# The second MLP product as seven block products in place of eight, with weight sums formed by accumulating DMAs

## The chip, the cores and the metric

One core of one Trainium2 chip runs the whole program. The metric is the time of the execution on the device in microseconds. The median of three runs of the kernel before is 1993.25 us (1992.52 to 1994.31).

## What is computed

Six layers work on 256 tokens of width 1024, in float32. Two come from a first block (three attention mixers side by side), four from a second (retention, conformer convolution, short convolution, retention). Each layer is a mixer and then an MLP that has the same shape in all six: 1024 to 4096, squared ReLU, 4096 back to 1024.

```python
# first block, for each of 2 layers
u = rmsnorm(x, ln2_g[layer]) @ w_up[layer]
x = x + jnp.square(jax.nn.relu(u)) @ w_down[layer]

# second block, for each of 4 layers
h = squared_relu_mlp(rms_norm(x, norm_g[i, 2]), mlp_w1[i], mlp_w2[i])
x = x + rms_norm(h, norm_g[i, 3])

def squared_relu_mlp(x, w1, w2):
    return jnp.square(jax.nn.relu(x @ w1)) @ w2
```

## The kernel before

**Precision.** Every large product is made of three matmuls. Each operand is split into a part `hi`, rounded to the type float32r, and a rest `lo`; the products hi·hi, hi·lo and lo·hi are summed in PSUM (`xs` and `ws`, lines 743 to 780). So a weight tile that has landed in a buffer `raw` is first cast by ScalarE (ACT) into `whi`, and VectorE (DVE) subtracts to get `wlo` (`prefetch`, lines 712 to 727). `hilo` (line 801) does the same for activations.

**Weights.** The host packs all weights into one tensor `in_w` in the order in which they are used (`plan`, line 69, and `pack`, line 1625), in units of up to 128 rows by 1024 columns, 512 KB each. SyncE issues one DMA for each unit. There are 4 buffers `raw` and 8 each of `whi` and `wlo`, each handed out in order (`CAPS`, line 41).

**The MLP** (`mlp`, line 1202). The token rows are two blocks of 128 (`t`), the output columns two halves of 512. The first four blocks of the hidden dimension come out with tokens on the partitions and are transposed. Then the loop over `p` from 2 to 15 runs: two units of the up projection give the hidden blocks 2p and 2p+1 with the hidden dimension on the partitions (`ws`, 48 matmuls of 256 columns into a PSUM bank `pu`); ReLU, square and hi/lo split follow on ACT and DVE; and the blocks 2p-4 and 2p-3 of the down projection are added up in four banks `acc` (`both`, 24 matmuls of 512 columns: 2 blocks x 2 token blocks x 2 column halves x 3). There are 14 such passes in each of six MLPs, 84 in all. `tail` (line 786) then does the last four hidden blocks, token block by token block and half by half, so that what follows a finished half (`Fin._half`, line 564: add to `x`, or a norm's sum of squares and gain) runs while the next half is being computed.

**PSUM.** Of eight banks four have the name `acc` and four `wk`.

**The order of the work.** The program is recorded first. A planner (`Rec.schedule`, line 389) then simulates all engines with the costs of `Rec.cost` (line 293), gives every instruction a due time from TensorE's order, and hands out buffers; the order that comes of this is emitted, one in-order stream for each engine (`Rec.emit`, line 536; so nearly all rows of the trace carry line 546). The planner's figures are its own; they are not measured times.

## Time and profile before

| | us |
|---|---|
| median of 3 runs | 1993.25 |
| span of the profiled execution, first to last instruction | 1991.4 |
| TensorE busy in it | 1949.0 (98%) |
| VectorE busy | 1335.8 (67%) |
| ScalarE busy | 1051.1 (53%) |
| GpSimd busy | 159.1 (8%) |
| moved by DMA | 341.44 MB, 52.6% of 16 engines' time on the main queue |

Only the span of the profiled execution is recorded, so times are set against the median by what lies between 1991.4 and 1993.25, 1.85 us. PE stands for the matmuls of TensorE, PEld for its loads of the stationary operand, DVE for VectorE, ACT for ScalarE, POOL for GpSimd, SP for SyncE, which issues the DMAs. Busy time is the union of an engine's instructions, so back-to-back matmuls of 394 ns each that overlap count less than their sum. `acc` and `wk` are PSUM banks; `t4k`, `r2k`, `s2k`, `s1k` are SBUF buffers of 4, 2, 2 and 1 KB on each partition.

### The profile page before, as it was taken

What the parts mean: (1) busy time and instruction counts of PE and PEld (TensorE: products, weight loads), DVE (VectorE), ACT (ScalarE), POOL (GpSimd) and SP (SyncE); (2) the same over time, 40 slices, a digit from 0 to 9 for tenths busy, and PEclk for the clock granted to TensorE, in tenths of its full rate; (3) what the DMA queues carried; (4) which work ended last, traced back from release to release, by engine and by line L of the source; (5) the groups of instructions that cost most, each with busy time, mean ns of one, the idle gap of its engine ahead of it and who ended that gap; (6) DMA issues with size and microseconds to landing.
All of it is one profiled execution on the core that took longest, in us unless ns stands there. A gap on an engine that the chain in (4) does not pass through costs nothing.

```text
span 1991.4 us, 30668 instructions
## 1 busy us (share of the span) xinstructions
PE 1949.0 (98%) x11696; PEld 1721.8 (86%) x11696; DVE 1335.8 (67%) x2169; ACT 1051.1 (53%) x1757; POOL 159.1 (8%) x233
## 2 busy tenths in 40 slices
PE   8999999999999999999997799999999999999998
PEld 7879998878998888899877689989899889888997
DVE  7866556886556776755589975567755577757554
ACT  7555545555545335645486655455545453555452
POOL 2200002100000000000047400000000000000000
PEclk9999999999999999999998899999999999999999
DMA  7256664246555555465631265646465655455552
GB/s 238 85 168 204 188 197 146 76 152 208 189 198 183 174 165 192 165 198 189 210 129 48 80 226 186 200 159 217 164 202 189 201 170 169 160 192 178 191 184 91
DMA packets 95763, 341.44 MB, mean 171 GB/s; under 512 B 10624, under 2 KB 10880, under 8 KB 95616
## 3 DMA queue, kind: packets, MB, share of 16 engines
q1 hardware_dynamic: 95616, 339.49, 52.6%
q8 instruction: 91, 1.49, 0.3%
q14 instruction: 56, 0.46, 0.1%
HBM read 338.40 MB, written 1.05 MB: 170 GB/s over the span
## 4 chain that ended last, share of the span: by engine, by line
PE 90%; DVE 6%; issue 1%; POOL 1%; DMA 1%; ACT 1%; SPq 0%; POOLq 0%; DVEq 0%; ACTq 0%
PE wk L546 47%; PE acc L546 43%; DVE s1k L546 4%; DVE s2k L546 1%; POOL s2k L546 1%; DMA raw<-in_w 1%; ACT s2k L546 0%; DVE wlo L546 0%; DMA x<-in_x 0%; DVE col L546 0%; DVE t4k L546 0%; DVE dg L546 0%; POOL s1k L546 0%; ACT whi L546 0%; SPq L546 0%
## 5 line engine op out<-in xcount | busy, mean ns | idle before, releaser
L546 DVE TENSOR_TENSOR wlo<-raw,whi 128x1024 fp32r<-128x1024 f32 (+3 forms) x639 | 774.0, 1217 | 538.2 <-ACT whi L546 533.6
L546 ACT CAST whi<-raw 128x1024 fp32r<-128x1024 f32 (+3 forms) x639 | 656.5, 1034 | 734.7 <-PE wk L546 374.5
L546 PE MATMUL wk<-t4k,whi 128*128 128x256 f32 x3712 | 662.8, 282 | 12.4 <-DVE s2k L546 8.8
L546 PEld LDWEIGHTS wk<-t4k,whi 128*128 128x128 f32 x3712 | 573.8, 190 | 22.0 <-DVE s2k L546 9.6
L546 PE MATMUL wk<-t4k,wlo 128*128 128x256 f32 x1856 | 510.7, 282 | 0.0
L546 PE MATMUL acc<-whi,r2k 128*128 128x512 f32 x1440 | 410.3, 394 | 0.0
L546 PE MATMUL acc<-whi,t4k 128*128 128x512 f32 (+2 forms) x1312 | 391.4, 387 | 5.9 <-ACT t4k L546 2.1
L546 PEld LDWEIGHTS wk<-t4k,wlo 128*128 128x128 f32 x1856 | 346.6, 190 | 0.1
L546 PEld LDWEIGHTS acc<-whi,r2k 128*128 128x128 f32 x1440 | 264.8, 188 | 54.6
L546 PEld LDWEIGHTS acc<-whi,t4k 128*128 128x128 f32 x1312 | 239.7, 189 | 48.5 <-ACT t4k L546 3.2
L546 PE MATMUL acc<-wlo,r2k 128*128 128x512 f32 x720 | 227.8, 393 | 0.0
L546 PE MATMUL acc<-wlo,t4k 128*128 128x512 f32 (+2 forms) x656 | 227.7, 386 | 0.0
L546 PE MATMUL wk<-whi,t4k 128*128 128x512 f32 x512 | 163.9, 398 | 0.0
L546 PEld LDWEIGHTS acc<-wlo,r2k 128*128 128x128 f32 x720 | 135.2, 188 | 31.1
L546 PEld LDWEIGHTS acc<-wlo,t4k 128*128 128x128 f32 x656 | 123.1, 190 | 20.1
L546 POOL TENSOR_TENSOR col<-col,mhalf 128x1 f32<-128x1 f32 (+1 forms) x48 | 38.3, 806 | 1157.1 <-DVE col L546 1156.8
L546 PEld LDWEIGHTS wk<-whi,t4k 128*128 128x128 f32 x512 | 95.8, 188 | 21.8 <-ACT t4k L546 0.4
L546 PE MATMUL wk<-wlo,t4k 128*128 128x512 f32 x256 | 98.7, 395 | 0.0
L546 PE MATMUL wk<-s2k,s2k 128*128 128x64 f32 (+6 forms) x492 | 85.3, 308 | 4.1 <-DVE s2k L546 3.6
L546 PEld LDWEIGHTS wk<-s2k,s2k 128*128 128x128 f32 (+2 forms) x492 | 72.6, 197 | 16.5 <-DVE s2k L546 4.0
L546 ACT ACTIVATE t4k<-wk,cv 128x128 fp32r<-128x128 f32 x256 | 72.4, 379 | 16.2 <-PE wk L546 15.9
L546 DVE SCALAR_TENSOR_TENSOR t4k<-wk,cv,t4k 128x128 fp32r<-128x128 f32 x256 | 72.4, 343 | 10.5 <-ACT t4k L546 9.6
(126 smaller groups left out, 1366.2 us busy)
## 6 DMA issues: line engine op xcount, KB each, us to landing
raw<-in_w SPq DMA_DIRECT2D x599, 512.0 KB, 4.2
raw<-in_w SPq DMA_DIRECT2D x26, 384.0 KB, 3.2
row<-in_rows SPq DMA_DIRECT2D x11, 512.0 KB, 5.0
raw<-in_w SPq DMA_DIRECT2D x8, 288.0 KB, 2.8
raw<-in_w SPq DMA_DIRECT2D x4, 432.0 KB, 4.8
kcs<-in_kc SPq DMA_DIRECT2D x2, 768.0 KB, 7.4
x<-in_x SPq DMA_DIRECT2D x4, 256.0 KB, 6.3
out_dram<-x SPq DMA_DIRECT2D x4, 256.0 KB, 2.0
```

Of the source, the lines that this page charges most:

```text
L546: op.dma = fn(*[res(a) for a in op.args], **{k: res(a) for k, a in op.kw.items()})
```

## The change

In the loop over `p` the pair of down blocks (2p-4, 2p-3) is no longer eight block products (two token blocks, two hidden blocks, two column halves) but seven, in Winograd's form of Strassen's algorithm. Each is three matmuls of 512 columns, 21 in place of 24. The seven results stay in seven PSUM banks over all 14 passes of an MLP (`strassen`), and are combined once at its end (`combine`, two copies and eight additions or subtractions). The last four hidden blocks still go through `tail` into four fresh banks, and what `combine` gave is added in `Fin` (`add`, `_half`).

The activations need four sums of the four blocks (`forms`); the blocks and sums, seven of 128 x 128, are split into hi and lo. The square is now taken on ACT.

The weights of a pair need seven forms of 128 x 512 each. `seven` makes them in one buffer `raw`: a DMA from SyncE loads two forms (512 KB), then DMAs issued by GpSimd with `accum_op=ALU.add` add further blocks of the weights to what lies in the buffer. Between these steps the buffer is split into `whi` and `wlo`, 1024, 1024, 1024 and 512 columns. There are four accumulating DMAs of 256 KB and one plain one of 256 KB beside the 512 KB load for each pair.

All eight banks get one name, `ps`. There are 6 buffers `raw`, handed out in any order, as `whi` and `wlo` now are; `dg`, the conformer's diagonal matrices, lie in `raw` buffers. The planner's costs change: matmuls by `n * 0.4434 + 4.5` ns, 1100 ns for a DMA issue on GpSimd, 4000 ns for a DMA in the due times, and the diagonals are made at most 6 us ahead.

```diff
@@ -29,6 +29,8 @@
 HALVED = 1
+DIAG_HOLD = 6000.0
+DMA_LAG = 4000.0
@@ -38,9 +40,9 @@
 SLACK = {}
-CAPS = {"raw": (4, True), "whi": (W_BUFS, True), "wlo": (W_BUFS, True), "t4k": (8, False), "row": (2, True),
+CAPS = {"raw": (6, False), "whi": (W_BUFS, False), "wlo": (W_BUFS, False), "t4k": (8, False), "row": (2, True),
         "s2k": (14, False), "r2k": (8, False), "s1k": (14, False), "col": (28, False), "keep": (20, False), "sm": (1, True),
-        "kcs": (1, True), "dg": (4, False), "acc": (4, False), "wk": (4, False)}
+        "kcs": (1, True), "ps": (8, False)}
...
@@ -62,7 +65,7 @@
     for p in range(2, 16):
-        out += u(p) + d(p - 2)
+        out += u(p) + [(down, l, (2 * p - 4, 2 * p - 3), SEVEN)]
...
@@ -295,7 +299,7 @@
             op.dma = n / 360.0
-            return 60.0, 2000.0
+            return (60.0 if op.eng == "sync" else 1100.0), 2000.0
@@ -305,7 +309,7 @@
             f32 = op.kw["lhsT"].vt.dtype == F32
-            return ((4 if f32 or n < 256 else 1) * max(n, P)) / 2.4 + 2.5, lat
+            return (4 * max(n, 64) / 2.4 + 5.0 if f32 else n * 0.4434 + 4.5), lat
@@ -331,10 +335,13 @@
         op.rush = self.rush
+        op.hold = self.hold
         op.label = sys._getframe(2).f_code.co_name if LABEL else ""
         items = [(k, a) for k, a in enumerate(args)] + list(kw.items())
         outs = [a for k, a in items if isinstance(a, V) and k in (0, "out", "accum_out")]
         ins = [a for k, a in items if isinstance(a, V) and k not in (0, "out", "accum_out")]
+        if "accum_op" in kw:
+            ins = ins + outs
@@ -380,7 +387,7 @@
                 q = ops[p]
-                lag = q.cost + (700.0 if q.dma else latency(q.eng, op.eng)) + q.dma
+                lag = q.cost + (DMA_LAG if q.dma else latency(q.eng, op.eng)) + q.dma
...
@@ -554,6 +561,17 @@
         self.parts = [[None, None], [None, None]]
+        self.part = None
+
+    def add(self, c):
+        net, nc = self.net, self.net.nc
+        if self.g is not None:
+            self.part = c
+            return
+        for t in range(2):
+            for hf in range(2):
+                x = net.x[t][:, hf * 512:hf * 512 + 512]
+                nc.vector.scalar_tensor_tensor(x, c[t][hf], self.scale[t], x, op0=ALU.mult, op1=ALU.add)
@@ -575,6 +593,10 @@
         else:
+            if self.part is not None:
+                y = self.part[t][hf]
+                nc.vector.tensor_add(y, y, p)
+                p = y
...
@@ -706,13 +728,16 @@
 
-    def ps(self, tag="wk"):
-        return VT(self.rec, tag, [P, 512], F32, True).view()
+    def ps(self):
+        return VT(self.rec, "ps", [P, 512], F32, True).view()
 
     def prefetch(self, upto):
         nc = self.nc
         while len(self.loaded) < min(upto, len(self.plan)):
             i = len(self.loaded)
+            if self.plan[i][3] is SEVEN:
+                self.loaded[i] = self.seven(i)
+                continue
@@ -726,10 +751,37 @@
 
+    def seven(self, i):
+        nc = self.nc
+        src = self.wpack[self.offs[i]:self.offs[i + 1]].rearrange("(p f) -> p f", p=P)
+        r = self.t("raw", [P, 1024])
+        out = []
+
+        def split(n):
+            hi = self.t("whi", [P, 1024], F32R)
+            lo = self.t("wlo", [P, 1024], F32R)
+            self.hilo(hi[:, :n], lo[:, :n], r[:, :n])
+            out.extend((hi[:, c:c + 512], lo[:, c:c + 512]) for c in range(0, n, 512))
+
+        nc.sync.dma_start(r, src[:, :1024])
+        split(1024)
+        for c in (slice(0, 512), slice(512, 1024)):
+            nc.gpsimd.dma_start(r[:, c], src[:, 1024:1536], accum_op=ALU.add)
+        split(1024)
+        nc.gpsimd.dma_start(r[:, :512], src[:, 512:1024], accum_op=ALU.add)
+        nc.sync.dma_start(r[:, 512:], src[:, 1536:2048])
+        split(1024)
+        nc.gpsimd.dma_start(r[:, :512], src[:, 1536:2048], accum_op=ALU.add)
+        split(512)
+        return out
+
     def unit(self, name, l, kbs):
         u = self.plan[self.wi]
         assert u[:3] == (name, l, tuple(kbs)), (u, name, l, kbs)
         self.prefetch(self.wi + 1 + LOOKAHEAD)
+        if u[3] is SEVEN:
+            self.wi += 1
+            return self.loaded[self.wi - 1]
@@ -783,11 +835,48 @@
 
-    def tail(self, items, acc, fin, first=False):
+    def forms(self, g):
+        nc = self.nc
+        e = self.t("s2k", [P, 4, P])
+        hi = self.t("t4k", [P, 7, P], F32R)
+        lo = self.t("t4k", [P, 7, P], F32R)
+        nc.vector.tensor_sub(e[:, 0:2, :], g[:, 0:1, :].to_broadcast([P, 2, P]), g[:, 1:3, :])
+        nc.vector.tensor_sub(e[:, 2, :], e[:, 1, :], g[:, 1, :])
+        nc.vector.tensor_add(e[:, 3, :], e[:, 2, :], g[:, 3, :])
+        self.hilo(hi[:, 0:3, :], lo[:, 0:3, :], g[:, 1:4, :])
+        self.hilo(hi[:, 3:7, :], lo[:, 3:7, :], e)
+        return [(hi[:, q, :], lo[:, q, :]) for q in range(7)]
+
+    def strassen(self, w, x, m, first, last):
+        f1, f5, f2, f6, f3, f7, f4 = w
+        xa1, xb2, xb1, s3, s1, s2, s4 = x
+        for b, (xh, xl), (wh, wl) in ((0, xa1, f1), (2, s4, f5), (4, s1, f2), (6, s3, f6), (5, s2, f3), (1, xb1, f7), (3, xb2, f4)):
+            self.mm(m[b], xh, wh, first, False)
+            self.mm(m[b], xh, wl, False, False)
+            self.mm(m[b], xl, wh, False, last)
+
+    def combine(self, m):
+        nc = self.nc
+        c = [[self.t("s2k", [P, 512]) for _ in range(2)] for _ in range(2)]
+        u2 = self.t("s2k", [P, 512])
+        u3 = self.t("s2k", [P, 512])
+        m1, m2, m3, m4, m5, m6, m7 = m
+        nc.scalar.copy(u2, m1)
+        nc.vector.tensor_add(u2, u2, m6)
+        nc.vector.tensor_sub(u3, u2, m7)
+        nc.vector.tensor_add(c[0][0], u3, m4)
+        nc.vector.tensor_sub(c[0][1], m5, u3)
+        nc.scalar.copy(c[1][0], m1)
+        nc.vector.tensor_add(c[1][0], c[1][0], m2)
+        nc.vector.tensor_sub(c[1][1], m5, u2)
+        nc.vector.tensor_add(c[1][1], c[1][1], m3)
+        return c
+
+    def tail(self, items, acc, fin, first=False, both=True):
         half = [slice(0, 512), slice(512, 1024)]
         for t in range(2):
             ts_ = slice(t * P, (t + 1) * P)
-            for hfs in ([(0, 1)] if first and t == 0 else [(0,), (1,)]):
+            for hfs in ([(0, 1)] if first and both and t == 0 else [(0,), (1,)]):
...
@@ -1204,7 +1293,7 @@
         px = [self.ps(), self.ps()]
-        h0 = [self.t("t4k", [P, 4, S], F32R) for _ in range(2)]
+        g0 = [self.t("s2k", [P, 4, P]) for _ in range(2)]
@@ -1213,26 +1302,38 @@
                 nc.tensor.transpose(pt[:, b * P:(b + 1) * P], r[:, b * P:(b + 1) * P], self.ident)
-            ts_ = slice(t * P, (t + 1) * P)
-            self.hilo(h0[0][:, :, ts_], h0[1][:, :, ts_], pt.rearrange("p (k n) -> p k n", k=4))
-        hT = {b: (h0[0][:, b, :], h0[1][:, b, :]) for b in range(4)}
-        acc = self.acc4()
+            for q in range(2):
+                for b in range(2):
+                    nc.scalar.copy(g0[q][:, 2 * b + t, :], pt[:, (2 * q + b) * P:(2 * q + b + 1) * P])
+        x = {q: self.forms(g0[q]) for q in range(2)}
+        m = None
+        hT = {}
         for p in range(2, 16):
             pu = self.ps()
             for j in range(2):
                 self.ws(self.unit(up, l, ALL), xT, pu[:, j * S:(j + 1) * S])
             r = self.t("s2k", [P, 512])
-            hh = self.t("r2k", [P, 512], F32R)
-            hl = self.t("r2k", [P, 512], F32R)
             nc.scalar.activation(r, pu, AF.Relu)
-            nc.vector.tensor_mul(r, r, pu)
-            self.hilo(hh, hl, r)
-            for j in range(2):
-                hT[2 * p + j] = (hh[:, j * S:(j + 1) * S], hl[:, j * S:(j + 1) * S])
-            for k in (2 * p - 4, 2 * p - 3):
-                self.both(self.unit(down, l, (k,)), [hT[k]], acc, k == 0)
+            if p < 14:
+                g = self.t("s2k", [P, 4, P])
+                nc.scalar.activation(g.rearrange("p a b -> p (a b)"), r, AF.Square)
+            else:
+                hh = self.t("r2k", [P, 512], F32R)
+                hl = self.t("r2k", [P, 512], F32R)
+                nc.vector.tensor_mul(r, r, pu)
+                self.hilo(hh, hl, r)
+                for j in range(2):
+                    hT[2 * p + j] = (hh[:, j * S:(j + 1) * S], hl[:, j * S:(j + 1) * S])
+            if m is None:
+                m = [self.ps() for _ in range(7)]
+            self.strassen(self.unit(down, l, (2 * p - 4, 2 * p - 3)), x.pop(p - 2), m, p == 2, p == 15)
+            if p < 14:
+                x[p] = self.forms(g)
+        c = self.combine(m)
+        acc = self.acc4()
         fin = mkfin(acc)
-        self.tail([(self.unit(down, l, (k,)), hT[k]) for k in range(28, 32)], acc, fin)
+        fin.add(c)
+        self.tail([(self.unit(down, l, (k,)), hT[k]) for k in range(28, 32)], acc, fin, first=True, both=False)
...
@@ -1408,7 +1509,8 @@
                 if (c, k0) not in kept:
-                    kept[c, k0] = dg = self.t("s2k" if n < S else "dg", [P, 4, P])
+                    self.rec.hold = DIAG_HOLD
+                    kept[c, k0] = dg = self.t("s2k" if n < S else "raw", [P, 4, P])
...
@@ -1627,6 +1730,11 @@
         w = inp[name][l]
+        if cs is SEVEN:
+            (a, b), h = kbs, 512
+            w = w.reshape(-1, P, 1024)
+            pieces.append(np.concatenate([w[a, :, :h], w[b, :, h:], w[a, :, h:], w[b, :, :h]], axis=1).ravel())
+            continue
...
```

## Rows read from the trace of the kernel before

**Rows 1.** The page, part 1: busy time of each engine, share of the span.

```profile
PE 1949.0 (98%) x11696; PEld 1721.8 (86%) x11696; DVE 1335.8 (67%) x2169; ACT 1051.1 (53%) x1757; POOL 159.1 (8%) x233
```

**Rows 2.** The page, part 4: the chain that ended last, by engine.

```profile
PE 90%; DVE 6%; issue 1%; POOL 1%; DMA 1%; ACT 1%; SPq 0%; POOLq 0%; DVEq 0%; ACTq 0%
```

**Rows 3.** That chain, last MLP: start us, us, what.

```profile
1822.12 5.55 PE acc L546 x24
1827.67 5.67 PE wk L546 x48
1833.34 5.52 PE acc L546 x24
...
1968.08 11.08 PE acc L546 x48
```

**Rows 4.** Waits of PE over the span: us in total, times, longest us.

```profile
PE wk L546 <- DVE s2k L546: 14.5, 4, 4.5
PE wk L546 <- DVE s1k L546: 8.4, 5, 3.7
PE wk L546 <- DMA x<-in_x: 4.6, 2, 4.0
```

**Rows 5.** Stretches: busy us by engine, clock, DMA share, GB/s.

```profile
core 0: us, PE busy (x) PEld busy (x) DVE busy (x) ACT busy (x) POOL busy (x), PEclk, DMA share, GB/s
8.00:16.00 8.00, 7.67 (x33) 6.49 (x34) 5.75 (x17) 7.26 (x20) 1.07 (x2) 1.00 1.02 404
630.00:720.00 90.00, 90.00 (x553) 80.41 (x552) 69.45 (x118) 39.85 (x56) 7.69 (x9) 1.00 0.53 175
...
990.00:1090.00 100.00, 87.42 (x517) 78.77 (x516) 90.86 (x136) 72.23 (x164) 56.32 (x64) 0.95 0.29 95
1160.00:1310.00 150.00, 150.00 (x965) 136.08 (x965) 86.65 (x89) 75.25 (x92) 0.20 (x4) 1.00 0.61 196
```

**Rows 6.** Instruction groups by shape: xcount, busy us, mean ns, idle before and releasers.

```profile
L546 DVE TENSOR_TENSOR wlo<-raw,whi 128x1024 fp32r<-128x1024 f32 x599 | 732.6, 1228 | 528.3 <-ACT whi L546 524.3 <-issue 1.9 <-PE wk L546 0.4
L546 ACT CAST whi<-raw 128x1024 fp32r<-128x1024 f32 x599 | 625.4, 1049 | 716.0 <-PE wk L546 374.5 <-PE acc L546 270.9 <-issue 42.5
...
L546 ACT ACTIVATE s2k<-wk 128x512 f32<-128x512 f32 x96 | 56.9, 593 | 18.5 <-PE wk L546 18.5
...
L546 ACT CAST r2k<-s2k 128x512 fp32r<-128x512 f32 x84 | 51.7, 615 | 0.8 <-DVE s2k L546 0.8
...
L546 DVE TENSOR_TENSOR r2k<-s2k,r2k 128x384 fp32r<-128x384 f32 x8 | 4.4, 552 | 0.0
...
L546 DVE TENSOR_TENSOR s1k<-s1k,wk 128x256 f32<-128x256 f32 x10 | 4.2, 420 | 0.7
...
L546 ACT COPY s2k<-wk 128x128 f32<-128x128 f32 x8 | 1.7, 268 | 1.0 <-PE wk L546 0.9
...
L546 DVE TENSOR_TENSOR s1k<-s1k,s1k 128x128 f32<-128x128 f32 x4 | 1.0, 276 | 0.0
```

**Rows 7.** DMA issues: xcount, KB each, median us to landing; whole span.

```profile
raw<-in_w SPq DMA_DIRECT2D x599, 512.0 KB, 4.2
...
out_dram<-x SPq DMA_DIRECT2D x4, 256.0 KB, 2.0
```

**Rows 8.** The same view, first 20 us.

```profile
raw<-in_w SPq DMA_DIRECT2D x3, 512.0 KB, 7.7
x<-in_x SPq DMA_DIRECT2D x4, 256.0 KB, 6.3
```

**Rows 9.** Timeline at an MLP's start: start us, us, instruction, idle before.

```profile
1155.12 0.59 ACT L546 ACTIVATE s2k<-wk 128x512 f32<-128x512 f32 x1
...
1156.96 0.68 DVE L546 TENSOR_TENSOR s2k<-s2k,wk 128x512 f32<-128x512 f32 x1
...
1159.63 0.68 DVE L546 TENSOR_TENSOR t4k<-wk,t4k 128x512 fp32r<-128x512 f32 x1
```

**Rows 10.** Timeline at the last MLP's end, in the same columns.

```profile
1984.72 0.69 DVE L546 TENSOR_TENSOR s2k<-acc,row 128x512 f32<-128x512 f32 x1 [1.07 <-PE acc L546]
1985.44 0.60 ACT L546 ACTIVATE s2k<-acc 128x512 f32<-128x512 f32 x1 [2.75 <-DVE s2k L546]
```

More of the change, by code (lines that the diff above doesn't have):

```diff
@@ L56 @@
 ONE = ((0, 1024),)
+SEVEN = ((0, 512), (512, 1024), "seven")
 W_O_ORDER = (3, 4, 5, 6, 7, 0, 1, 2)
@@ L113, in unit_size @@
 def unit_size(u):
-    return len(u[2]) * sum(b - a for a, b in u[3])
+    return len(u[2]) * sum(c[1] - c[0] for c in u[3] if c != "seven")
 PRE = ["ln1_0", "ln1_1", "ln2_0", "ln2_1"] + [f"n{i}_{q}" for i in range(4) for q in (0, 2)]
@@ L259 @@
     __slots__ = ("i", "eng", "name", "args", "kw", "vts", "preds", "succs", "cost", "lat", "dl", "start", "end", "nleft",
-                 "est", "dma", "label", "rush", "rows")
+                 "est", "dma", "label", "rush", "rows", "hold")
 class Eng:
@@ L289, in __init__ @@
         self.rush = False
+        self.hold = None
         for n in LAT:
@@ L394, in schedule @@
             op.nleft = len(op.preds)
-            hold = AHEAD if op.eng == "sync" and op.vts[0].tag != "raw" else HOLD
+            hold = op.hold or (AHEAD if op.eng == "sync" and op.vts[0].tag != "raw" else HOLD)
             op.est = max(0.0, op.dl - hold)
@@ L639, in along @@
         for t in range(2):
-            dg = net.t("dg", [P, P])
+            dg = net.t("raw", [P, P])
             nc.scalar.activation(dg, net.ident, AF.Copy, scale=self.get(kind, t))
@@ L849, in acc4 @@
     def acc4(self):
-        return [[self.ps("acc") for _ in range(2)] for _ in range(2)]
+        return [[self.ps() for _ in range(2)] for _ in range(2)]
     def setup(self):
@@ L1036, in group @@
             kss = TRIPLES if name == "vckr" else PAIRS
-            acc = [self.ps("acc") for _ in range(2)]
+            acc = [self.ps() for _ in range(2)]
             ws = [None] * len(kss)
@@ L1087, in block1_mixer @@
         for t in range(2):
-            banks = [self.ps("acc") for _ in range(2)]
+            banks = [self.ps() for _ in range(2)]
             for k in range(3):
@@ L1103, in block1_mixer @@
         for t in range(2):
-            banks = [self.ps("acc") for _ in range(2)]
+            banks = [self.ps() for _ in range(2)]
             self.xs(w, cTk[3:], [b[:, :384] for b in banks], 2, True, True, t)
@@ L1282, in do_v @@
         def do_v(h):
-            acc = [self.ps("acc") for _ in range(2)]
+            acc = [self.ps() for _ in range(2)]
             ws = [None] * 4
@@ L1419, in conv @@
                                        cv[:, w:w + nd][:, :, None].to_broadcast([P, nd, P]))
+                    self.rec.hold = None
                 dg = kept[c, k0]
```

## The prediction

> **What bounds the kernel now.** I read the share of busy time first: TensorE 98%, nothing else above 67% [rows 1]. A busy share alone does not say that PE sets the end, so I read the chain next: 90% of what ended last is PE, and only 6% DVE [rows 2]. In the last MLP the chain is matmuls and nothing else: 24 matmuls of the down product, 5.52 to 5.55 us, then 48 of the up product, 5.67 us, over and over, 13 such pairs from 1822.12 to 1968.08, then the tail's 48 in 11.08 us [rows 3]. That is 145.96 / 13 = 11.23 us for one pass, and 11.08 / 48 = 0.231 us for one 512-column matmul. Where PE does wait, the largest three causes are 14.5, 8.4 and 4.6 us in all [rows 4]; they lie in the attention and conformer stretches and at the first load. In a whole MLP loop PE is busy 150.00 of 150 us at the full clock, 1.00 (2.4 GHz), with DVE 58%, ACT 50%, POOL 0.1% and the DMA engines at 61% for 196 GB/s [rows 5]. So in the loop a matmul removed is time removed, as long as all the other engines still fit into the shorter pass.
>
> **What is removed.** 3 of 24 matmuls per pass: 3 x 0.231 = 0.69 us, so 11.23 becomes 10.54. 14 passes in 6 MLPs: 84 x 0.692 = 58.1 us, 2.9%. The number of PE instructions must fall by 252, to 11444.
>
> **DVE and ACT in a pass.** Both get much more work. The pass needs five splits of 1024 columns (2 up units, 3 of `seven`) and one of 512. DVE: 5 x 1.228 [rows 6] + 0.69 for the 512, as the subtraction of that width takes 0.68 [rows 9], plus `forms`: 0.42 + 2 x 0.28 for the sums and 0.55 + 0.69 for the two rests [rows 6]: 9.05 us, 86% of 10.54. ACT: 5 x 1.049 + 0.615, ReLU 0.593 and a square of the same size, casts 0.51 + 0.615 for the forms (0.51 between the 128- and 512-wide rows): 8.2 us, 78% [rows 6]. Neither is the bound. Their load has a price, though, since both run in a fixed order. Bounds from rows: with DVE at 77% PE lost nothing (90.00 of 90 us), and with DVE at 91% it lost 12.6%, but in a stretch where DVE is itself the producer of PE's next operand in a chain [rows 5]. The MLP's weights are made ahead, so I go by the first row and take 1% of a pass, 0.1 us, times 84 = 8.4 us; the ends are 0 and 0.6 us a pass (half of what the second row would give).
>
> **The DMA engines.** A pass moved 4 units of 512 KB, 2.10 MB in 11.23 us = 187 GB/s; the rows show 196 [rows 5]. Now it moves 2 up units, 512 KB, one plain and four accumulated pieces of 256 KB: 2816 KB = 2.88 MB in 10.54 us = 274 GB/s. No row shows an accumulating DMA. Lower bound: it costs what a plain one of its size does, 274 GB/s. Upper bound: the bytes of the target, which have to be read too, count like transferred ones: 1.05 MB more, 3.93 MB, 373 GB/s. The engines have shown 404 GB/s when full, from 8 to 16 us [rows 5]; 196 GB/s at 61% would make it 321. At 404 even the upper bound takes 9.73 us and fits into 10.54; at 321 it takes 12.25 and doesn't. I take the 404, because it is a row of the engines actually full, while 61% holds idle latencies of single packets. So the forecast has DMA at 68 to 92% busy, and no cost.
> The Trainium skill speaks against this part. In "Collectives: The Full Stack", section "The bandwidth ceiling: the fold count and why AG ≠ RS ≠ AR", it says that an add in the DMA datapath needs two source reads on one ring and so runs at about half the rate of a copy. By it the upper bound holds, not the lower; the sum stays as it is at 404 GB/s, and the second rival below is what it becomes at 321. No trace here shows it yet.
>
> **The queue of GpSimd.** POOL issues four accumulating DMAs per pass and has 0.1% of work there now [rows 5]. No row shows its price for an issue. From below: the SP issues that show no busy time at all, so 0; from above, what fills the pass: 10.54 / 4 = 2.6 us each. POOL's only other work near by is the `pow` of a norm at a stage's end, which waits behind an issue that waits for its split; I put that at nothing in the middle and in the next item at the ends.
> The Trainium skill, "DMA: Bandwidth & Descriptors", section "SWDGE vs HWDGE vs iDMA", says that an accumulating DMA can only be issued from GpSimd, whose software builds the descriptors, and its specifications give about 1 us to the first byte. By that POOL would be under half busy and the sum would not change.
>
> **The chain in one unit.** Load, split, add, split, add, split, add, split: each add waits for DVE's last read, each cast for the landing. With a split at 1.05 + 1.23 = 2.3 us and an add at `a`, one step is d = 2.3 + a. What must hold is the count of buffers. PE takes the four tiles of a unit within 4.85 us, but they become ready d apart, so the early ones are held: 3d - 0.5, 2d + 0.9, d + 2.3 and 2.1 us, and the two up tiles 5.1 us each; together 6d + 15 us in a pass. Eight buffer pairs offer 8 x 10.54 = 84 us, so d may be 11.5 and `a` 9.2 us. The rows give 2.0 us (256 KB out, quiet), 4.2 (512 KB), 6.3 and 7.7 us (crowded start) for a landing [rows 7, 8]: all below 9.2. The six `raw` buffers offer 63 us and are needed 25.5 + 3a, so `a` may be 12. The chain has room, if the emitted order spaces the steps by about what they take; it is fixed ahead by a planner that does not know the landing times.
>
> **Ends of the loop.** At the start ReLU, square, transpose, copy out and split take 1155.12 to 1160.31 for the first token block, much of it behind other work [rows 9], and stand against 5.67 us of `pu` matmuls. New in this path: four copies of 0.27 for one cast of 0.59, sums of 0.42 + 2 x 0.28, each with a hand-over, about 1.8 us more. The first product needs no sum, which hides 0.7. I take 1 us exposed at each of six MLPs, bounds 0 and 2: 6 us. At the end `combine` puts 7 x 0.68 on DVE, beside the first 5.5 us of the tail, whose first group has a free bank. The addition of the part in `_half` looks like 0.69 us more in the chain after the last matmul, but today DVE reads the bank for 0.69 and only then ACT for 0.60 [rows 10]; with the sum in SBUF the two follow it side by side, so the chain keeps its length. I take 0.7 us per MLP for the crowding, bounds 0 and 1.5: 4 us. The pool of eight banks and the new planner costs can also move the other stages; of the 28 us that PE waits there [rows 4] I expect none back, with -5 and +5 us as ends.
>
> **Sum.** 1991.4 - 58.1 + 8.4 + 6 + 4 = 1951.7 us of span; the profiled span lies 1.85 us below the median, so 1953.5 us.
>
> **Rival 1: the weights come late (slower).** The fixed order puts the cast that follows an add at a place in ACT's stream; if the add lands later than planned, ACT stands still, and behind it wait the casts of the up units and ReLU, behind those DVE's rests, and PE. It decides from a stall of (58.1 - 10) / 84 = 0.57 us a pass: only 5% of a pass eats the whole gain. At 0.8 us a pass the time is 1993.25 - 48.1 + 67 = 2012 us. For it: a chain of seven steps where there was one, DVE at 86%, and ACT's waits are for the engine before it already now [rows 6]. Against: 84 us of buffer time for about 54 us of need at a = 4.2.
>
> **Rival 2: the DMA engines are the bound (slower).** At 321 GB/s and with the target's bytes counted, a pass takes 12.25 us: 84 x (12.25 - 11.23) = +86 us, and +10 for the ends: 2089 us. It decides from 11.1 us a pass, 354 GB/s. For it: 61% busy at 196 GB/s. Against: 404 GB/s shown. A mild form between gives 2000 to 2030.
>
> **Rival 3: it gains nothing that can be seen.** If the compute is as said, but the loop settles on a pass near 11.1 us because splits and adds lock step with PE, what is left is within a few us of 1993: 1985 to 1997.
>
> **How the numbers follow.** 0.2% is 4 us, about what a measurement of this kernel can tell from no change. Forecast (1935 to 1985): 0.66; rival 1: 0.16; rival 2: 0.10; rival 3: 0.08, of which about a third counts as faster, most of the rest as no change. Faster 0.69, same 0.07, slower 0.24. The range starts at 1934 (no stall at all and a few us back elsewhere) and reaches to 2015, which takes in rival 3 and most of rival 1 and leaves out the heavy form of rival 2 and the tail of the first. The forecast's own range is 1935 to 1985.
>
> **What would show it.** Right: 11444 PE instructions; passes of 48 + 21 matmuls in the chain at about 10.6 us; DVE near 86% and ACT near 78% of the loop; POOL queue transfers of 256 KB landing in under 7 us; PE waits per MLP of a few us, at its start. Wrong: PE waiting on `whi` or `wlo` inside the loop, or a clock below 1.00 there, which I do not reckon with; a DMA share near 1.00 in the loop (rival 2); ACT idle before casts with the DMA as the releaser while the share is well below 1.00 (rival 1); gaps over 2 us at the ends of the MLPs.

## The result and the profile after

The changed kernel takes 2167.43 us, median of four runs (2163.71 to 2174.98); the kernel before, measured beside it, 1993.78 us. The ratio is 1.0879, 95% interval 1.0866 to 1.0891: 174 us slower, where 40 us faster was forecast. The forecast missed by 214 us and its range by 152.

First the busy times of the changed kernel (the page, part 1), to be set against [rows 1].

```profile
span 2164.9 us, 32295 instructions
PE 1982.9 (92%) x11444; PEld 1706.6 (79%) x11444; DVE 1567.6 (72%) x2667; ACT 1255.3 (58%) x2141; POOL 452.5 (21%) x569
```

The matmuls are gone, 11444 as forecast, yet PE is busy 34 us longer and idle 182 us (2164.9 - 1982.9) where it was idle 42. The mean granted clock explains part of the longer busy time:

```profile
core 0: 2164.9 us, clock 0.971
```

It was 0.991 before. At two levels, 1.2 and 2.4 GHz, 0.971 means that 0.029 x 2 x 2164.9 = 126 us ran at 1.2 GHz, against 36 us before; the added stretches follow PE's own gaps (PE is busy 5.29 of the 7.30 us from 2006 to 2013.3, and from 2013.3 to 2016.5 the clock is 0.50). Next the chain of work that ended last, by engine and by line, against [rows 2], where PE had 90%:

```profile
PE 34%; issue 28%; DMA 22%; DVE 8%; POOL 4%; ACT 3%; POOLq 0%; SPq 0%; ACTq 0%; DVEq 0%
PE ps L553 34%; DMA raw<-in_w 21%; DVE s1k L553 3%; POOL raw L553 3%; DVE wlo L553 3%; ACT whi L553 2%; DVE s2k L553 1%; POOL col L553 1%; ACT s2k L553 1%; DVE t4k L553 1%; POOL s2k L553 1%; DVE x L553 1%; DVE col L553 0%; DMA x<-in_x 0%; POOL s1k L553 0%
```

PE's matmuls are now a third of the chain; the landings of weights are 22%, and 28% is `issue`, time for which this view names no releaser. Over 500 of its 609 us stand right before a DMA that GpSimd issues, as in these rows of the chain (start us, us, what); the timeline further down names VectorE's `wlo` as what the issue at 2021.59 waited for.

```profile
2016.87 4.70 issue
2021.57 0.01 POOLq L553
2021.59 4.37 DMA raw<-in_w
```

The waits (us in total, times, longest) of ACT and PE show the same: ACT's first one, which was for PE before, and PE's first three, against [rows 4].

```profile
ACT whi L553 <- DMA raw<-in_w: 332.5, 155, 5.6
PE ps L553 <- DVE wlo L553: 72.1, 101, 1.4
PE ps L553 <- DVE s2k L553: 52.7, 12, 6.8
PE ps L553 <- ACT whi L553: 21.8, 24, 4.0
```

ACT stands still before casts because a DMA has not landed; PE then waits for `wlo` a hundred times, inside the loops, about 0.7 us each. Two MLP loops as windows (columns as in [rows 5]):

```profile
1936.00:2133.00 197.00, 179.30 (x1034) 153.30 (x1033) 131.38 (x188) 117.91 (x181) 47.60 (x56) 0.96 0.85 213
1553.00:1728.00 175.00, 154.91 (x928) 134.66 (x926) 115.63 (x162) 105.14 (x151) 44.41 (x53) 0.96 0.89 221
```

PE is busy 88 to 91% there at a clock of 0.96; before it was 100% at 1.00 [rows 5]. A pass of the loop takes 12.3 to 13.5 us (medians of the six MLPs, from the first up matmul to the next pass's), not the forecast's 10.5. Neither DVE (67%) nor ACT (60%) is full. The DMA engines are at 0.85 to 0.89 (the first stretch begins before its loop; inside the six loops they are at 0.87 to 0.93), for only 213 to 221 GB/s. Last the DMA issues (xcount, KB each, median us to landing), against 4.2 us in [rows 7]:

```profile
raw<-in_w SPq DMA_DIRECT2D x515, 512.0 KB, 5.2
raw<-in_w POOLq DMA_DIRECT2D x336, 256.0 KB, 6.3
raw<-in_w SPq DMA_DIRECT2D x86, 256.0 KB, 3.5
```

A 256 KB add takes longer to land than a 512 KB load.

**How late landings become lost time.** The order that the planner fixed counts 1.3 us, 0.7 us of transfer and 0.7 us for such an add (lines 518, 301 and 533 of the changed kernel): 2.7 us. In it ACT casts, one pass after another, the second 1024 columns of unit u, then the first 1024 of unit u+1; after DVE's rests GpSimd issues the third sum of u and the pair of adds for u+1; the next such casts wait for that pair. GpSimd's and ACT's timelines (start us, us, what, idle before) show one turn of this:

```profile
2009.22 0.86 POOL L553 DMA_DIRECT2D raw<-in_w  x1 [5.89 <-DVE wlo L553]
2010.35 1.75 POOL L553 DMA_DIRECT2D raw<-in_w  x2 [0.27 <-DVE wlo L553]
2016.23 0.88 POOL L553 DMA_DIRECT2D raw<-in_w  x1 [4.13 <-DVE wlo L553]
2021.59 0.88 POOL L553 DMA_DIRECT2D raw<-in_w  x1 [4.47 <-DVE wlo L553]
2022.72 1.76 POOL L553 DMA_DIRECT2D raw<-in_w  x2 [0.26 <-DVE wlo L553]
...
2018.98 2.00 ACT L553 CAST whi<-raw 128x1024 fp32r<-128x1024 f32 x2 [3.35 <-DMA raw<-in_w]
```

The pair issued at 2010.35 releases ACT at 2018.98, 8.63 us later; two casts of 2.00 together, DVE's rest and the issue follow, and the next pair goes out at 2022.72: a period of 12.37 us, 8.63 of it landing. The chain of waits of an earlier MLP (start us, us, what) is the same turn seen from its end:

```profile
1706.66 9.33 DMA raw<-in_w x2
1715.99 0.02 issue
1716.01 0.04 ACTq L553
1716.05 0.04 issue
1716.09 1.06 ACT whi L553
1717.14 0.02 issue
1717.17 1.24 DVE wlo L553
1718.40 0.28 issue
1718.69 6.53 DMA raw<-in_w
```

With some 3.8 us of the period that is not landing, this order keeps up with TensorE's 10.5 us only if a pair lands within 6.7.

### The profile page after: what moved, and what is told of

The parts are those of the page before. It is cut to its first block, busy times and chain, and to the rows that moved or that the text cites. A ratio compares the mean times of both kernels' runs of the same rounds, so it can differ in the third digit from the quotient of the medians.

```text
span 2164.9 us, 32295 instructions
## 1 busy us (share of the span) xinstructions
PE 1982.9 (92%) x11444; PEld 1706.6 (79%) x11444; DVE 1567.6 (72%) x2667; ACT 1255.3 (58%) x2141; POOL 452.5 (21%) x569
## 3 DMA queue, kind: packets, MB, share of 16 engines
q0 software_dynamic: 48384, 88.10, 25.7%
## 4 chain that ended last, share of the span: by engine, by line
PE 34%; issue 28%; DMA 22%; DVE 8%; POOL 4%; ACT 3%; POOLq 0%; SPq 0%; ACTq 0%; DVEq 0%
PE ps L553 34%; DMA raw<-in_w 21%; DVE s1k L553 3%; POOL raw L553 3%; DVE wlo L553 3%; ACT whi L553 2%; DVE s2k L553 1%; POOL col L553 1%; ACT s2k L553 1%; DVE t4k L553 1%; POOL s2k L553 1%; DVE x L553 1%; DVE col L553 0%; DMA x<-in_x 0%; POOL s1k L553 0%
## 5 line engine op out<-in xcount | busy, mean ns | idle before, releaser
L553 DVE TENSOR_TENSOR wlo<-raw,whi 128x1024 fp32r<-128x1024 f32 (+2 forms) x807 | 917.7, 1161 | 465.8 <-ACT whi L553 458.7
L553 ACT CAST whi<-raw 128x1024 fp32r<-128x1024 f32 (+2 forms) x807 | 779.0, 991 | 668.4 <-DMA raw<-in_w 332.5
L553 PE MATMUL ps<-whi,t4k 128*128 128x512 f32 (+2 forms) x2808 | 896.8, 395 | 19.4 <-ACT whi L553 13.5
L553 PE MATMUL ps<-t4k,whi 128*128 128x256 f32 x3712 | 696.9, 291 | 49.3 <-DVE s2k L553 41.0
L553 PEld LDWEIGHTS ps<-t4k,whi 128*128 128x128 f32 x3712 | 599.1, 198 | 63.3 <-DVE s2k L553 44.9
L553 PEld LDWEIGHTS ps<-whi,t4k 128*128 128x128 f32 x2808 | 523.1, 189 | 139.3 <-ACT whi L553 29.1
L553 PE MATMUL ps<-wlo,t4k 128*128 128x512 f32 (+2 forms) x1404 | 539.6, 397 | 43.0 <-DVE wlo L553 43.0
L553 PE MATMUL ps<-t4k,wlo 128*128 128x256 f32 x1856 | 532.5, 293 | 29.5 <-DVE wlo L553 29.1
L553 POOL DMA_DIRECT2D raw<-in_w x336 | 293.5, 951 | 1109.0 <-DVE wlo L553 1024.4
L553 PEld LDWEIGHTS ps<-t4k,wlo 128*128 128x128 f32 x1856 | 361.6, 198 | 41.2 <-DVE wlo L553 40.7
L553 ACT ACTIVATE t4k<-ps,cv 128x128 fp32r<-128x128 f32 x256 | 72.5, 377 | 17.0 <-PE ps L553 15.8
```

Source lines behind the costliest of these rows:

```text
L553: op.dma = fn(*[res(a) for a in op.args], **{k: res(a) for k, a in op.kw.items()})
```

## The experiments

The first theories. **A**: only the order is wrong; it was made for landings of 2.7 us, and even plain copies, which land in 4 to 5, would spoil it. **B**: the add itself is dear; its second read fills the DMA engines and makes everything land late. **C**, added after the first runs: the lock-step turn above, through the pair. All times stand beside runs of the kernel before on the same chip (medians of 1992.6 to 1993.6 us). A landing or pass length given without a row is a median over the trace's issues and matmuls.

### Adds or copies, old order or a longer lead

**e1_plain**: the order untouched, the DMAs copy.

```diff
-            op.dma = fn(*[res(a) for a in op.args], **{k: res(a) for k, a in op.kw.items()})
+            op.dma = fn(*[res(a) for a in op.args], **{k: res(a) for k, a in op.kw.items() if k != "accum_op"})
```

> The changed kernel with its instruction order untouched, but the four DMAs per pass that GpSimd issues copy instead of add (the weight sums are left out, so the block products use wrong weights). Theory A, the order: the planner spaces the steps of the weight chain by an add that lands in 2.7 us, and they land in 6.3 (median); plain copies from the same queue still take some 4 us or more, so passes stay above 11.7 us and the time above 2070. Theory B, the DMA engines: an add's 2 KB packet costs 205 ns on an engine where a plain one costs 107; 11.8 us of packets per pass in place of 8.7. With copies the engines have room again: passes of 10.6 to 10.9 us, 1950 to 1980 us.

1974.05 us, ratio 0.9912 (0.9884 to 0.9939). The same bytes through the same order: 193 us less. Its page, parts 1 and 3, its last loop as a window, and part 3 of the changed kernel (queue, kind: packets, MB, share of 16 engines):

```profile
PE 1910.4 (97%) x11444; PEld 1678.0 (85%) x11444; DVE 1567.8 (79%) x2667; ACT 1259.7 (64%) x2141; POOL 340.8 (17%) x569
q0 software_dynamic: 26880, 88.10, 14.3%
1826.00:1950.00 124.00, 122.34 (x810) 111.70 (x809) 100.34 (x132) 90.66 (x124) 22.96 (x43) 1.00 0.78 262
```

```profile
q1 hardware_dynamic: 95616, 317.47, 42.4%
q0 software_dynamic: 48384, 88.10, 25.7%
```

GpSimd's queue moves 88.10 MB in both. As copies that takes 0.143 x 1972.5 = 282 us of all 16 engines, as adds 0.257 x 2164.9 = 556 us: 1.97 times. The adds go out in packets of 2 KB, the copies in packets of 4 KB, but the size is not what costs: by the traces' packets a 2 KB packet takes 178 ns (median) as an add and 84 as a plain load of SyncE, a 4 KB packet 159. Landings of this queue fall from 6.3 to 4.9 us, passes to 10.55 us. Of the 192.4 us between the two spans 120 are idle time of PE, and 72.5 are more busy time for the same matmuls. All of it lies in the six MLP loops: from a loop's first up matmul to its last, all six together, they take 1068 us in the changed kernel, 876 in e1 and 912 before. Theory A alone falls.

**e2_replan** lets the planner count 3500 ns more for a GpSimd DMA (called a longer lead below); everything is computed. **e3_replan_plain** does both edits.

```diff
-                op.end = max(op.end, dma_at)
+                op.end = max(op.end, dma_at) + (3500.0 if e == "gpsimd" else 0.0)
```

> The changed kernel, computing the same, but the planner reckons 3.5 us more for a DMA issued by GpSimd (landing after 6.2 us in place of 2.7), so the order gives the adds more lead. Theory A: PE's waits in the loop go; passes of 10.6 to 10.9 us, 1950 to 1985 us. Theory B: the engines stay full with 11.8 us of packets per pass; passes of 11.6 to 12.5 us, 2030 to 2110 us, and the landing times grow.

> Both together: the order planned for 6.2 us, and copies in place of adds (the weight sums are left out). Theory A: as the replanned kernel, within 10 us of it. Theory B: 1950 to 1980 us, at least 60 us below the replanned kernel with adds. If it stays above 2030, neither is the cause, and the load of DVE and ACT (86 and 78% of a pass) is.

2062.04 us (ratio 1.0344, 1.0328 to 1.0359) and 1977.42 us (0.991, 0.9887 to 0.9933). A longer lead takes back 105 us of the 193 with all adds in place, and nothing where the DMAs are copies. So neither cause stands alone. In all three runs the time falls where theory B put it, but B does not say why the order is worth 105 us beside adds. Eight passes inside a loop, of the changed kernel, e2 and e1:

```profile
517.00:616.50 99.50, 90.10 (x554) 77.05 (x553) 68.58 (x94) 63.43 (x89) 27.83 (x32) 1.00 0.93 231
1507.00:1599.50 92.50, 85.91 (x554) 77.33 (x555) 70.34 (x96) 63.33 (x88) 27.86 (x32) 1.00 1.00 260
486.00:570.40 84.40, 84.40 (x554) 77.02 (x553) 70.28 (x97) 65.04 (x90) 17.43 (x33) 1.00 0.83 280
```

In e2 the DMA engines are full and PE is not: 92.5 us for eight passes are 11.56 us a pass, all of it engine time. The changed kernel holds the same, 0.93 x 99.5 / 8 = 11.57 us a pass, but spreads it over 12.4; the copies hold 0.83 x 84.4 / 8 = 8.8. At these packet times four adds do not fit into the 10.55 us of TensorE, whatever the lead. Full engines alone cost 84 x (11.56 - 10.55) = 85 us, and e2, at 11.5 to 12.2 us a pass (medians of the six MLPs), is near that; its six loops take 960 us, 84 more than e1's. The other 108 us, from 960 to 1068, are what the changed kernel's order adds.

**e10_replan60** is e2 with 6000 in place of 3500.

> Everything is computed as in the changed kernel, but the planner is told that a DMA from GpSimd lands 6000 ns later than it thought (3500 ns gave 2062 us). If the fixed order is all that binds, the longer lead covers the 8.5 us of the slow adds too and the passes fall to the planner's 10.7 to 11.3 us: 1985 to 2020 us. If the DMA engines are full (their share was 0.90 to 0.93 at 3500 ns), more lead brings little: 2045 to 2070 us with the share staying at 0.90 or more in the loops.

2125.39 us (1.0671, 1.0643 to 1.0699), worse than with 3500: neither branch. Three units are now in flight at a time; from a unit's first add to its last landing go 37.6 us (31.0 in e2, 25.8 in the changed kernel), so that unit's `raw` buffer is held as long. Whether the six buffers are what binds was not tried.

### Which add, and the load beside it

**e8_pair_copy** makes the pair copies, **e9_others_copy** the other two; the order is untouched (the line of `emit` that drops `accum_op` where a DMA is so marked is not shown).

```diff
-            nc.gpsimd.dma_start(r[:, c], src[:, 1024:1536], accum_op=ALU.add)
+            nc.gpsimd.dma_start(r[:, c], src[:, 1024:1536], accum_op=ALU.add, copy=True)
```

> The order is untouched; only the pair of adds on the 1024-column buffer (the first two of the four) become plain copies of the same 256 KB each, and the other two stay adds. Left out: the second operand of those two sums. Theory C (a lock-step cycle: cast of a unit, VectorE's subtraction, issue of the pair, landing of the pair 8.0 to 9.5 us later, next cast): with a pair of copies landing in about 5 us the cycle falls to some 9 us, below TensorE's own 10.5, so passes of 10.6 to 11.0 us and 1975 to 2010 us. Theory B (the total load of the DMA engines counts, whichever add it is): half of the extra load of the adds is gone, so half of the 193 us between the changed kernel (2167) and its copy version (1974) comes back, some 2050 to 2090 us.

> The order is untouched; the pair of adds stays, the two later adds of 256 KB become plain copies. Left out: the second operand of those two sums. The number of added packets taken away is that of the run where the pair is made a copy. Theory C (lock-step through the pair's landing): the pair still lands some 7.5 to 8.5 us after its issue, so passes of 11.8 us or more and at least 2090 us. Theory B (total load): the same time as with the pair as copies, some 2050 to 2090 us in both.

2087.06 us (1.0467, 1.045 to 1.0485) and 2105.92 us (1.0572, 1.0546 to 1.0598). B is right about e8 and C about e9, and each is wrong about the other: freeing the pair alone does not free the pass. **e6_half_up** halves the columns of the up units' loads and leaves adds and order alone (again one line of several).

```diff
-                nc.sync.dma_start(raw[:, c], src[:, c])
+                    nc.sync.dma_start(raw[:, c], src[:, c], half=True)
```

> The changed kernel with its order and its adds untouched, but the loads of the up projection's units bring only half of their columns (256 KB in place of 512 KB; the rest of the tile holds what was there). That takes 16 x 159 ns, 1.3 us for each of two units, half of it, from each DMA engine: about 1.3 us of packets per pass. Theory B (the engines are too full, so adds queue behind the up loads): the adds land earlier than 6.3 us in the median, passes of 10.6 to 11.3 us, 1975 to 2050 us. If the add itself is slow whatever runs beside it, or the order alone binds, passes stay at 12.4 us or more and the time above 2120 us.

2115.49 us (1.0606, 1.0581 to 1.063): 52 us less, between the two theories. The three and e1 share one order, so the turn can be checked in all (medians in us; a landing goes from the first issue of the pair to the later landing, a pass here from one pair's issue to the next pair's):

```
kernel          pair lands   pass    pass less landing
changed            8.87      12.87        4.00
e9_others_copy     8.46      12.41        3.95
e6_half_up         8.28      12.24        3.96
e8_pair_copy       7.75      12.05        4.30
e1_plain           6.07      10.46        4.39 (PE is the limit)
```

So the turn of C is there, pass = landing + 4, and single turns show it more sharply: the next pair goes out 3.7 to 3.9 us after a landing in 67 of the changed kernel's 78 turns inside MLPs, in 66 of e9's, 64 of e6's, 47 of e8's and 31 of e1's. What C had wrong is what makes the pair late. The third sum of the unit before is issued 1.1 us ahead of the pair (2009.22 and 2010.35 above): three transfers of 256 KB in one burst beside the loads of SP. As copies the pair still shares the engines with that add and lands only 1.1 us earlier. Lateness is common to all in the burst (B); the order turns it into passes, one for one.

### Other ways to make the sums

**c1_dve**: the pair's sums by VectorE, from an extra 256 KB load, lead 3500. **e4_pool_add**: all four by GpSimd from SBUF, no accumulating DMA. **c2_pool**: the pair by GpSimd, lead 3500.

The pair's line in c1 and in e4 (c2's is c1's with `nc.gpsimd`; the loads into further buffers are not shown):

```diff
-            nc.gpsimd.dma_start(r[:, c], src[:, 1024:1536], accum_op=ALU.add)
+            nc.vector.tensor_add(r[:, c], r[:, c], q[:, :512])
```

```diff
-            nc.gpsimd.dma_start(r[:, c], src[:, 1024:1536], accum_op=ALU.add)
+            nc.gpsimd.tensor_add(r3[:, c], r1[:, c], r2[:, :512])
```

> Same result. The first two of the four sums of a pair (one 256 KB block added to two others) are made by DVE from a plainly loaded block, 2 x 0.68 us, only the last two by accumulating DMAs; the planner reckons 6.2 us for these. Packets per engine and pass: 10.2 - 16 x 0.178 + 8 x 0.084 = 8.0 us. Theory B: passes of 10.6 to 10.9 us, 1960 to 1990 us, if DVE at 10.4 of 10.54 us can hold that; if DVE is then the bound, passes of 11 to 11.5 us, 2005 to 2050 us.

> Same arithmetic, but the weight sums are made in SBUF by GpSimd: two plain loads of 512 KB per pair as before, four additions of 512 columns (1.66 us each by a row of before, 6.6 us per pass) between three buffers. No add in a DMA, 2.1 MB per pass in place of 2.9. Theories A and B both: passes of 10.6 to 10.9 us, 1950 to 1985 us. If DVE and ACT are what is too full, or DVE slows down beside GpSimd's reads, passes stay above 11.2 us, over 2000 us.

> The same with GpSimd for the first two sums, 2 x 1.9 us. Theory B: the DMA engines have room as in the kernel with DVE; DVE is slowed by GpSimd's reads for about a third of their time, 1.3 us per pass, so 10.3 of 10.54 us. Passes of 10.6 to 11.0 us, 1960 to 2000 us; if the chain by GpSimd takes too long, over 2030 us.

2022.72 (1.0151, 1.0127 to 1.0175), 2153.07 (1.0799, 1.0783 to 1.0815) and 2090.74 us (1.0482, 1.045 to 1.0515). e4 moves no byte twice, and is nearly as slow as the changed kernel, with its DMA engines at a share of only 0.51 (509 to 611.4 us, inside a loop); two of its groups (busy, mean ns, idle before), against the 1228 ns of [rows 6]:

```profile
L553 DVE TENSOR_TENSOR wlo<-raw,whi 128x1024 fp32r<-128x1024 f32 x683 | 954.4, 1407 | 243.8 <-ACT whi L553 239.2 <-PE ps L553 0.2
L553 POOL TENSOR_TENSOR raw<-raw,raw 128x512 f32<-128x512 f32 x252 | 484.2, 1934 | 680.0 <-DVE wlo L553 505.9 <-DMA raw<-in_w 138.7 <-DVE col L553 12.0
```

GpSimd's additions take 1934 ns each, and DVE's rests are 15% longer beside them. The Trainium skill, "SBUF — State Buffer", section "Who interferes with whom", says that a VectorE instruction with two SBUF inputs contends with a GpSimd instruction that reads SBUF; the row agrees. What bounds these versions is not shown: VectorE is busy 85% of that stretch of e4 and 89% of a loop of c1 (480 to 600 us), whose DMA engines are at 0.87; neither is full.

### What is left of the miss

Copies brought 1974, not 1953.5. **e5_rest** keeps all of the change but the seven products (single PSUM name, six buffers, planner costs; its edit is long and not shown). **e11_before_costs** is the kernel before with only the planner's costs changed.

```diff
-            return 60.0, 2000.0
+            return (60.0 if op.eng == "sync" else 1100.0), 2000.0
...
-            return ((4 if f32 or n < 256 else 1) * max(n, P)) / 2.4 + 2.5, lat
+            return (4 * max(n, 64) / 2.4 + 5.0 if f32 else n * 0.4434 + 4.5), lat
...
-                lag = q.cost + (700.0 if q.dma else latency(q.eng, op.eng)) + q.dma
+                lag = q.cost + (DMA_LAG if q.dma else latency(q.eng, op.eng)) + q.dma
```

> The changed kernel without its core: the down product as before (eight block products, plain weights, four banks), but one pool of eight PSUM banks, six raw buffers in any order, diagonals in raw buffers and the new planner costs. Theory B (the adds load the DMA engines): what is left does next to nothing, passes of 11.2 us, 1985 to 2000 us. If the copies kernel's 1974 us, 20 above the forecast, hides a cost of these parts, this one comes out at 2003 to 2015 us.

> The kernel before, with nothing changed but the planner's costs that the change brings: matmul costs by n * 0.4434 + 4.5 ns, 1100 ns for a DMA issue on GpSimd, 4000 ns for a DMA in the due times. All is computed as before, with the old PSUM names, 4 raw buffers in order and the diagonals in buffers of their own. The changed kernel without its seven products took 2016.7 us, 23 us over the kernel before. If the costs are what lost them: 2008 to 2018 us. If the single PSUM name and the shared raw buffers lost them: 1990 to 1998 us.

2016.65 us (1.0114, 1.0097 to 1.0131) and 2018.89 us (1.013, 1.0113 to 1.0147). The planner's costs alone lose the kernel before 25 us, about as much as all that surrounds the seven products (e5, 23). **e12_old_plain** gives the copy version the costs of before; **e13_old_lead_plain** adds the lead of 3500.

> The changed kernel with copies in place of all adds (left out: the second operand of the four weight sums), and with the planner's costs of the kernel before (matmuls, DMA issue, 700 ns for a DMA in the due times); the seven products, the single PSUM name and the buffers are those of the change. With the new costs it took 1974 us. If those costs are the rest of the miss, what they lose in the kernel before (2019 against 1994, 25 us) comes back: 1945 to 1958 us, the forecast's own number with adds that are free. If they do not matter beside the seven products: 1968 to 1980 us.

> Copies in place of all adds (left out: the second operand of the four weight sums), the planner's costs of the kernel before, and 3500 ns more for a GpSimd DMA. Without the longer lead it took 2035 us. If the order made for landings of 2.7 us is what made those 2035 us: 1948 to 1965 us, the forecast's number when the adds are free and the order fits. If the old costs themselves hurt beside the seven products: 1990 us or more.

2035.48 us (1.0217, 1.0196 to 1.0238) and 1984.48 us (0.9958, 0.9943 to 0.9973). Neither reached 1953. The old costs without a lead spoil the order even for copies, with the lead they bring nothing (1977.42 without them). So the 25 us are shown for the kernel before; that the same 25 us are the rest of the miss beside seven products is not.

### A version that beats both

The fourth sum is of two halves that both lie in the buffer already, so it needs no DMA. **c3_fourth** leaves it to VectorE, lead 3500; **c3_fourth_old** has the planner's costs of before as well; **c4_dve_old** is c1 with those costs; **c7_fourth_old50** is c3_fourth_old with a lead of 5000.

```diff
-        nc.gpsimd.dma_start(r[:, :512], src[:, 1536:2048], accum_op=ALU.add)
+        nc.vector.tensor_add(r[:, :512], r[:, :512], r[:, 512:])
```

> The same sums as in the changed kernel and a planner that counts 3500 ns more for a GpSimd DMA (2062 us as such), but the fourth sum is made by VectorE, from two halves that both lie in the buffer already, so 84 adds of 256 KB are gone: a quarter of the added packets, 10752 of 178 ns over 16 engines, 120 us of engine time, 1.4 us a pass. VectorE gets 84 additions of some 550 ns. If full DMA engines are what is left at 2062 us: loop share below 0.85, passes of 10.7 to 11.1 us, 2010 to 2030 us. If the order binds (the pair still lands 8 us after its issue): 2045 us or more.

> The fourth sum by VectorE, 3500 ns more for a GpSimd DMA, and the planner's costs of the kernel before. If the costs are worth 25 us here too: 25 us less than with the new costs, 1985 to 2005 us. If the old costs plan passes too short for TensorE (9.8 us) and so bring weights late: no gain, 2010 us or more.

> The first two sums by VectorE, the last two by adds, 3500 ns more for a GpSimd DMA, and the planner's costs of the kernel before. With the new costs it took 2023 us. If the costs are worth 25 us here too: 1992 to 2003 us, level with the kernel before. If not: 2015 us or more.

> The fourth sum by VectorE, the planner's costs of the kernel before, and 5000 ns more for a GpSimd DMA in place of 3500 (1977 us). If the engines have room now, more lead covers the adds that land late: 1960 to 1975 us. If buffers or the engines bind as with all four adds at 6000 ns: 1980 us or more.

2003.45 (1.0052, 1.0037 to 1.0067), 1977.17 (0.9915, 0.99 to 0.9931), 2026.57 (1.0166, 1.0151 to 1.0182) and 1970.7 us (0.9884, 0.9867 to 0.99). One add less of four is worth 59 us against e2, more than either branch of the expectation. The old costs bring 26 more here and nothing in c4. The last one computes all and is 1.2% faster than the kernel before; its page, part 1, and one loop:

```profile
PE 1900.5 (96%) x11444; PEld 1673.9 (85%) x11444; DVE 1617.5 (82%) x2751; ACT 1257.2 (64%) x2141; POOL 390.2 (20%) x485
480.00:600.00 120.00, 120.00 (x789) 109.60 (x788) 104.00 (x141) 88.14 (x122) 27.04 (x31) 1.00 0.96 257
```

PE is busy 120.00 of 120 us at the full clock, with DMA engines at 0.96 and adds that still take 6.2 us to land. Three adds hold 0.96 x 10.55 = 10.1 us of engine time a pass, which fits. Nearly full engines are thus no loss in themselves, if the order leaves time for what lands late.

## Why the prediction was wrong, step by step

**TensorE's part held.** 252 matmuls are gone, and where weights come in time a pass takes 10.55 us (e1) for 10.54 forecast. So the gain of a pass is real. Summed over the six loops less comes of it: of the 54 us that the 78 products between a loop's first and last up matmul would save, e1 saves 36 (912 to 876) and c7 44 (to 868); the changed kernel's take 156 more than before.

**DVE and ACT held.** 86% and 78% of a pass were forecast; e1's loop shows 100.34 and 90.66 of 124 us, 81% and 73%, and PE loses 1.3% there for 1% forecast. GpSimd's issues also stayed inside their bounds: 0.86 to 0.88 us each for an add in the timeline above, GpSimd 21% busy in all.

**The DMA term failed, and with it the forecast.** The prediction put the bound of 3.93 MB against 404 GB/s, found 9.73 us, which "fits into 10.54", and took "no cost". The bound's idea was right: 1.97 times the engine time for the same bytes. The rule of the Trainium skill quoted there, in "Collectives: The Full Stack", section "The bandwidth ceiling: the fold count and why AG ≠ RS ≠ AR" (told there of a collective's reduce, whose add runs at about half the rate of a copy), agrees with it. Two things were wrong. First the rate. The 404 GB/s came from plain loads at the kernel's start; in the loop the 3.93 MB take 11.56 us of every engine (e2, share 1.00), 340 GB/s. The 321 that the prediction turned down was the nearer one. So a pass with four adds does not fit into 10.54; with three it does (10.1, c7), and with copies (8.8). Second, "fits" was made to mean "costs nothing", when landings are later on fuller engines: SyncE's 512 KB loads land in 4.2 us before, where the loops' share was 0.53 to 0.61 [rows 5, 7], and in 4.7 in e1, 4.8 in e2 and 5.2 in the changed kernel (not in step with the share: e2's is the highest). This term of 0 us measured 193 between the changed kernel and e1: by the split above 84 from full engines and 108 from late landings in the order as planned.

**The chain's allowance was taken from the wrong resource.** Buffers would allow a landing of 9.2 us, the prediction said, and all rows were below. So were all but 14 of the 336 landings of adds: 6.3 us median, 8.87 for a pair. But the condition it named itself, "if the emitted order spaces the steps by about what they take", was the one that decided: the order allowed 6.7. That the planner counts 2.7 us for a landing, where [rows 7] have 4.2 for a load, could have been read beforehand from its lines in the kernel; the 6.7 show only in the trace after.

**Rival 1 and rival 2 are each half right.** The marks of rival 1 (ACT idle before casts, with the DMA as releaser) and of rival 2 (high DMA share) appear together. Rival 2's 12.25 us a pass and 2089 us come nearest, 78 us short. Its reason, throughput, holds as a floor (11.56 us measured for its 12.25) and accounts for e2; it does not account for the changed kernel, whose engines are at 0.93 and whose passes follow the landing of the pair. Rival 1 set its price at 0.8 us a pass; what the order adds is 108 / 84 = 1.3, and the two together 193 / 84 = 2.3. The two were held apart, as chances of 0.16 and 0.10, when one feeds the other.

**The clock was left out knowingly.** "a clock below 1.00 there, which I do not reckon with": it was 0.96 in the two stretches above, with PE's gaps among the matmuls. e1's mean clock, 0.989, is 43 us at 1.2 GHz, the changed kernel's 126; work that fills the 83 us between would take half of that at 2.4 GHz, so by this estimate some 40 of the 72.5 us of longer busy time are the clock's. The rest is open: in the row of 517 to 616.5 us the clock is 1.00, and the 554 matmuls that take e1 84.4 us are busy for 90.1.

**The other stages: -5 to +5 us was too narrow.** e5 and e11 put the new planner costs at 23 to 25 us for the kernel before. The ends of the MLPs (10 us forecast) look about right: PE's waits for DVE's `s2k` grow from 14.5 [rows 4] to 27.5 us in e1.

**Open.** Why a lead of 6000 is worse than 3500 with four adds; and why the old costs gain 26 us in one version, nothing in two and lose 61 in a fourth. The orders differ in many places at once, and single steps of them were not tried. Nor is it shown what bounds the versions with sums by VectorE or GpSimd.

## What to carry to other kernels

Price a transfer by a row of the same mix in the same kind of stretch, not by the best rate that any row shows: here the choice between 321 and 404 GB/s decided the forecast. And a transfer that fits is not free: ask at what share the engines will then stand, how late a transfer lands at that share, and how late the fixed order lets it land; the smallest of these allowances counts, not the number of buffers. Where an order is planned ahead, read the planner's own figure for a new kind of operation first, for a wrong one is paid on every turn of the loop. Before an accumulating DMA, look whether both operands lie in SBUF already: that one sum, moved to an engine with room, together with a longer planned lead and the old costs, made the difference between 2167 and 1971 us.

## What the runs showed of the hardware beyond that

- An accumulating DMA from HBM into SBUF took 1.97 times the engine time of a copy of the same bytes, and GpSimd was busy 0.95 us on average for its issue (0.86 to 0.88 for one that stands alone) against 0.54 us for a copy's (the two groups of issues below, changed kernel and e1_plain: busy, mean ns).

```profile
L553 POOL DMA_DIRECT2D raw<-in_w x336 | 293.5, 951 | 1109.0 <-DVE wlo L553 1024.4 <-DMA raw<-in_w 45.1 <-DVE t4k L553 12.1
```

```profile
L553 POOL DMA_DIRECT2D raw<-in_w x336 | 180.9, 540 | 1035.8 <-DVE wlo L553 965.2 <-DMA raw<-in_w 38.0 <-DVE t4k L553 12.1
```

- With four additions of 512 columns on GpSimd in each pass (1934 to 2000 ns each) VectorE's 1024-column subtractions took 1407 ns in place of 1228, and the kernel ended only 14 us below the one with four adding DMAs.
- Packets in these traces took (medians) 178 ns for 2 KB of an accumulating DMA, 84 ns for 2 KB of a plain load by SyncE and 159 ns for 4 KB of a plain one, by either queue. Eight passes with four such DMAs each (e2, 92.5 us) kept all 16 DMA engines busy (share 1.00) at 260 GB/s of moved bytes.
